# Squares of x at eight late steps, input weights tied behind the last key/value copy, and four smaller moves in a hybrid attention layer

## The chip, the cores and the metric

One core of a Trainium2 chip. The time is device microseconds of one execution, as the median of several runs. The engines are TensorE (PE: matmuls, and PEld: their weight loads), VectorE (DVE), ScalarE (ACT), GpSimd (POOL), and SyncE (SP), which here only issues DMAs. Each engine takes its instructions in one fixed order and waits at the head of its queue.

## The reference

One encoder layer on x of 1024 positions by 1024 channels, float32. Two groups of attention heads read one projection; a gated convolutional feed-forward follows.

```python
hn = rms_norm(x, norm1_g)
proj = hn @ w_in                  # [qA 512 | kA 128 | vA 128 | qB 512 | kB 512 | vB 512]
qa = apply_axial_rope(rms_norm(qa, qa_norm_g), tables)
ka = apply_axial_rope(rms_norm(ka, ka_norm_g), tables)
out_a = global_gqa_attention(qa, ka, va)                # dense, 8 query and 2 kv heads
out_b = dilated_mixture_attention(rms_norm(qb, qb_norm_g), rms_norm(kb, kb_norm_g), vb)
mixed = concatenate([rms_norm(out_a, outa_norm_g), rms_norm(out_b, outb_norm_g)])
x = x + mixed @ w_out
x = x + conv_ffn(rms_norm(x, norm2_g), w_up, conv_w, conv_b, w_down)
```

`rms_norm` divides by the root of the mean of squares, so the squares of all of x are needed before a value of the projection can be scaled. `dilated_mixture_attention` is three patterns of strided windows for eight heads.

## The kernel before

All operands lie in two large SBUF areas (`bigf` for plain float32, `bigr` for the rounded parts that go to the PE) and one PSUM area (`ps`); the profile names only these three. A float32 product is made of three matmuls of 512 columns: high by high, high by low, low by high (L461 to L463). So each operand is first split: a high part by an ACT copy, and the low part by a DVE subtraction (`split`, L261 and L262, for x and its sums; `w_prep`, L446 to L450, for weights).

The stages follow one another on the PE: the input projection (to about 185 us of the trace), dense attention of group A (16 groups g of heads and positions, to about 388 us), the dilated heads of group B, the output projection, the up-projection with its convolution, and the down-projection.

**Projection.** First the key and value columns of group A: eight tiles of positions (`kv_proj`), four PSUM banks in turn, each copied out of its bank by ACT (`kv_out`, L335) and stored. Then 14 products (two halves of the columns, each as a seven-product scheme of 2 x 2 blocks, in the order 1, 5, 2, 3, 6, 7, 4 and 1, 5, 2, 6, 7, 4, 3), each over four slices k: 56 units m, and `in_unit(m)` issues twelve matmuls. Products 3, 5, 6, 7 take sums of blocks of x, which `x_sum` (DVE, L290 to L294) makes and `s_split` splits. `w_prep(m + 4)` stands behind unit m; its parts go to a ring of six buffers, so a weight's high copy waits for the PE to be done with the weight six places ahead.

**Mean of x.** `n_load` loads a tile of 128 rows of x (512 KB) into one buffer, `F_ROPE`; `n_sq` squares it on ACT with a running sum (L300). There is one such buffer, so a load can start only when the square before it is done. Behind the eighth square, `mean_x` makes the norm's factor. The key heads of group B are then normed, in two sets of four tiles (`done("kb", 0, u)` and `done("kb", 4, u)`): a square on ACT (L523; the first set's square goes to `F_ROPE`, the second's to part of the query area), a sum over each head on DVE (L526), a root, its refinement on DVE, a product (L541), and a store to `kscr`.

**Dense attention.** For each g and each pair of key blocks the PE makes scores (L796, L797), ACT takes the exponential (L802), ACT or DVE copies the high part (L806, L804), DVE subtracts for the low part (L807), and the PE multiplies by the values (L781). Between them stand steps of other work by a table `spread` (which g, which step): the rotary steps of the remaining query heads (`roped`; POOL L544 and L549, DVE L554 and L557) and the norms of group B's queries (`rest`, with the square at L577). By g, too, the first dilated heads' keys are loaded (`load_k`, from `kscr`), split (`b_split_k`, ACT L901 and POOL L902), and the outputs scaled (`scale_load` L835, `scale_a` L838).

**Dilated heads.** For each head, over 4 steps of a counter n: scores (L1038, L1039), DVE and ACT work around them (L1047, L1051), then `b_move`, two SP DMAs that put a head's outputs into the layout for the norm (L1087).

**What sets the order.** A scheduler gives each engine its queue from program order and dependences. `tc.issue_after(ins)` lets the instructions made inside it stand, on the engine of `ins`, only behind `ins`. It binds nothing on other engines. `last_exp`, `last_low` and the new `kv_last` are such instructions.

Of the kernel before, what the change touches and what calls it, by code (L numbers as in the profile page):

```python
# [15 lines left out]
AF = mybir.ActivationFunctionType  # L16
# [132 lines left out]
def tile_encoder_layer(ctx, tc, x, xT, w_in, w_kv, consts, norm2_g, w_out, w_up, convs,  # L149
# [17 lines left out]
    def emit(bounded):  # L167
# [32 lines left out]
        def bank(i, n=512, o=0):  # L200
            return PS[:, 512 * i + o:512 * i + o + n]
# [113 lines left out]
        def kv_bank(tt):  # L315
            return tt % 4
# [15 lines left out]

        def kv_out(i):
            stg = f(F_UA + 256 * i if i < 4 else F_W[1] + 1536 + 256 * (i % 2), 256)
            act(stg, bank(kv_bank(i), 256), AF.Copy)  # L335
            dma(kvscr[i], stg)

        def k4(o, j, n=64, off=0):
            return fp(o + 128 * j + off, [1024, 4], [64, 2], [1, n])
# [428 lines left out]
        def a_main_bounded(g, prep, tail, late, plan, late_plan):  # L768

            b, kv = grp(g)  # L770
            q2 = R_Q2A + 512 * (g % 2)
            ob = 6 + g % 2
            slots = {}

            def pv(j):
                ph, pl = slots[j]
                for u in range(2):
                    kt = 2 * j + u
                    v = R_VA + 132 * kt + 66 * kv
                    for i, (w, p) in enumerate(((v, ph), (v + 1056, ph), (v, pl))):  # L780
                        mm(bank(ob)[0:66], r(w, 66), r(p + 512 * u, 512), start=(kt == 0 and i == 0), stop=(kt == 7 and i == 2))  # L781

            def last():
                pv(3)
                vec.tensor_copy(f(F_OT, 512)[0:66], bank(ob)[0:66])
                for u in range(2):
                    dma(f(qab(b) + 256 * kv, 256)[64 * u:64 * u + 64].rearrange("p (c n) -> p c n", c=2),
                        fp(F_OT + 128 * u, [256, 2], [1, 128])[0:64])
                    dma(dna[u:u + 1, b, 256 * kv:256 * kv + 256].rearrange("o (c n) -> o c n", c=2),
                        fp(F_OT + 128 * u, [256, 2], [1, 128])[64:65])  # L790

            for j in range(4):
                st = 2 * (j % 2)
                for u in range(2):
                    kt = 2 * j + u
                    mm(bank(st + u), r(R_K2A + 1024 * kv + 128 * kt, 128), r(q2, 512), start=True, stop=False)  # L796
                    mm(bank(st + u), r(R_KHA + 1024 * kv + 128 * kt, 128), r(q2, 512), start=False, stop=True)  # L797
                n = pairs[0]
                pairs[0] += 1
                p, ph, pl = F_PB[n % 3], R_PHB[j], R_PLB[j]  # L800
                slots[j] = ph, pl
                last_exp[0] = act(f(p, 1024), bank(st, 1024), AF.Exp).ins  # L802
                if j == 1:
                    vec.tensor_copy(r(ph, 1024), f(p, 1024))  # L804
                else:
                    act(r(ph, 1024), f(p, 1024), AF.Copy)  # L806
                last_low[0] = vec.tensor_tensor(r(pl, 1024), f(p, 1024), rf(ph, 1024), op=OP.subtract).ins  # L807
                for kt in (2 * j, 2 * j + 1):
                    take(prep, plan[kt])
                    take(late, late_plan[kt])  # L810
                    now = f(F_PB[(n - 1) % 3], 1) if 0 < kt < 7 and g > 1 else \
                        rf(R_Q2A + 512 * ((g + (kt == 7)) % 2), 1)
                    for step in spread.pop((g, kt), []):
                        step(now)
                step = tail.pop(0) if tail else None
                if step:
                    step()
                if j > 2:
                    pv(j - 3)

            return [lambda: pv(1), lambda: pv(2), last]
# [520 lines left out]
        def at(m, fn, *a):  # L1342
            steps[m].append(lambda: fn(*a))

        for i in range(2, 8):
            at((4, 5, 7, 8, 10, 11)[i - 2], n_sq, i)
            if i < 7:
                at((4, 5, 7, 8, 10, 11)[i - 2], n_load, i + 1)
        at(11, mean_x)
        at(18, dma, f(F_ROPE, 1024), rope)  # L1350
        at(5, dma, f(O_OG, 240), convs)
# [35 lines left out]
        for m in range(4 * len(prods)):  # L1387
            c, n = prods[m // 4]
            if m < 52:
                in_unit(m)  # L1390
            else:
                for k in range(4):
                    in_unit(52 + k, [m - 52])
                in_out(13, m - 52)
                in_last = nc.cur_bb.bb.instructions[-1]
            if m % 4 == 3 and m < 52:
                for t in range(4):
                    in_out(m // 4, t)
            if m == 2:
                for i in range(4):  # L1400
                    kv_tile(i)
            if m == 3:
                for i in range(4, 8):
                    kv_tile(i)
                    if i % 2:
                        n_sq(i // 2 - 2)
                        n_load(i // 2 - 1)
            w_prep(m + 4)
            for s in steps.pop(m, []):
                s()  # L1410
        assert not steps
# [5 lines left out]
        if bounded:  # L1417

            def hold(o, now):
                vec.scalar_tensor_tensor(f(o, 1), now, 0.0, f(o, 1), op0=OP.mult, op1=OP.add)  # L1420

            def run(ts, o=None):
                def at(now):
                    if o is not None:
                        hold(o, now)
                    with tc.issue_after(in_last):
                        for t in ts:
                            t()
                return [at]

            tick = [lambda now: vec.tensor_copy(f(F_KN[0], 1), now)]
            for ts, at in zip(roped, (((0, 2), (1, 4), (1, 6)), ((2, 2), (3, 2), (3, 4)), ((3, 6), (4, 4), (4, 6)))):
                spread[at[0]] = tick + run(ts[:-2])
                spread[at[1]] = run(ts[-2:-1], F_KN[0])
                spread[at[2]] = run(ts[-1:], F_RS)
            for i, d in enumerate(rest):
                square_at, mean_at, root_at, refine_at, norm_at, gain_at = done(*d, i)
                spread[5 + i, 2] = [square_at]
                spread[5 + i, 7] = [mean_at]
                if i == 3:  # L1440
                    spread[9, 3] = [root_at]
                    spread[9, 7] = [refine_at]
                spread[10 + i, 0] = [norm_at]
                spread[11 + i, 2] = [gain_at]
        else:
            for s in sum(roped + [done(*d) for d in rest], []):
                s()
# [5 lines left out]
        if not bounded:  # L1453
# [5 lines left out]
        tail = []  # L1459
        prep = []  # L1460
        SM_A, SM_B = SM_T, SM_T + 64
        dense_late = {8: [(recip_load, 0)], 9: [(recip, 0), (scale_load, 0), (scale_load, 1), (scale_load, 2)],
                      11: [(scale_a, 0), (scale_load, 3)], 12: [(squares, 0, 0, 0, 0), (scale_a, 1)],
                      13: [(squares, 1, 0, 0, 1), (scale_a, 2)], 14: [(squares_sum, (0, 1), 0, SM_A), (squares, 2, 0, 0, 2), (scale_a, 3)],
                      15: [(squares, 3, 0, 0, 3)]}
        for g in range(16):

            prep += a_prep(g + 1) if g < 15 else []
            if g == 14:
                prep += [lambda: b_split(0)] + sum(sum(b_prep(0), []), [])  # L1470
            plan = {0: (1, 0, 1, 0, 0, 0, 0, 0), 14: (1, 1, 1, 0, 0, 0, 1, 1), 15: (1, 1, 0, 1, 0, 0, 0, 0)}.get(g, (0, 1, 0, 0, 1, 0, 0, 0)) if bounded else {14: (1, 1, 1, 1, 1, 2, 2, 2), 15: (2, 2, 2, 2, 1, 1, 1, 1)}.get(
                g, (1, 1, 1, 1, 1, 1, 1, 0))
            tail = a_main(g, prep, tail, late, plan, (0, 2, 2, 2, 1, 1, 1, 1))
# [10 lines left out]
            if g == 9:  # L1484
                load_tee(0, 0)
                load_tee(0, 1)
                load_tmx(1)
            if bounded:
                for fn, *a in dense_late.get(g, []):
                    with tc.issue_after(last_exp[0] if fn is squares else last_low[0]):  # L1490
                        fn(*a)
            if g == 11:
                load_k(0)
            if g == 13:
                load_k(1)
            if g == 10 and bounded:
# [49 lines left out]
        def dilated():  # L1546
# [11 lines left out]
            for n in range(32 + 4):  # L1558
# [14 lines left out]
                        b_recip(6)  # L1573
                    wo_load(5)
                h1, i1 = divmod(n - 7, 4)
                if h1 >= 0 and i1 == 0:
                    b_move(h1)
                h1, i1 = divmod(n - 3, 4)
                if 0 <= n - 3 < 32:
# [10 lines left out]
                if n < 32:  # L1590
# [19 lines left out]
                        step(1, "k0")  # L1610
                    for a, k in (((1, "k1"),), ((1, "q0"), (2, "split_k")), ((1, "q1"), (2, "split_q")), ((2, "k0"),))[i]:
                        step(h + a, k)
                    if n == 3:
                        for c, v in ((64, 1.0), (130, 0.0)):
                            fill(rp(R_VBB[1] + c, [132, 8], [1, 2]), 8, 2, v)
# [9 lines left out]
                if n == 34:  # L1625
                    with tc.issue_after(copied[0]):
# [1 line left out]
                    newton(f(SM_A + 16, 8), f(SM_A, 8), f(SM_A + 8, 8), f(SM_A + 24, 8))  # L1628

        dilated_late = {3: [(squares_sum, (2, 3), 0, SM_A)], 4: [(recip_load, 1)], 8: [(recip, 1)], 9: [(scale_load, 4)], 10: [(scale_load, 5)], 11: [(scale_load, 6)],  # L1630
                        13: [(scale_a, 4)], 14: [(scale_a, 5), (scale_a, 6)], 15: [(scale_load, 7)],
                        18: [(squares, 4, 0, 1, 0), (scale_a, 7)], 21: [(squares_sum, (4,), 1, SM_A)],
                        22: [(squares, 5, 0, 1, 0), (scale_b, 0)], 25: [(squares_sum, (5,), 1, SM_A)],
                        26: [(squares, 6, 0, 1, 0)], 29: [(squares_sum, (6,), 1, SM_A), (mix_split, 0, 0)],
# [660 lines left out]
```

## Time and profile before

| | us |
|---|---|
| three runs | 1169.40, 1170.62, 1173.34; median 1170.62 |
| profiled execution, own time | 1171.02 |
| its span in the trace | 1169.1 |
| PE busy in 0 to 50 / 50 to 160 / 160 to 240 | 47.33 / 110.00 / 78.20 |
| PE busy in 240 to 400 / 400 to the end | 158.92 / 763.39 |

The profiled execution's own time is 1.9 us more than its span, for what lies ahead of the first and behind the last instruction. The trace gives for each instruction its start, its length, its line and, in brackets, how long its engine sat idle before it and what ended that. Lengths of one engine's neighbours overlap a little, since a start is taken before its predecessor has fully drained.

### The profile page before, as it was taken

The numbers are of one execution on the slowest core, as the hardware profiler recorded it, in microseconds if no ns is written. First come the engines' busy times: TensorE is split into PE (matmuls) and PEld (weight loads), VectorE is DVE, ScalarE is ACT, GpSimd is POOL, SyncE is SP. The second block draws the span as 40 slices with busy tenths as digits, with TensorE's granted clock in tenths as the row PEclk, the third lists the DMA queues.
The fourth block names the chain that finished last, engine by engine and source line by source line (L and its number), as shares of the span: only waits on it lengthen the run. The fifth ranks groups of instructions, "written<-read, shape, count | busy, mean of one in ns | idle before, by whom it ended". The sixth has DMA issues, their size and how long they took to land.

```text
span 1169.1 us, 16273 instructions
## 1 busy us (share of the span) xinstructions
PE 1157.8 (99%) x5736; PEld 954.6 (82%) x5736; DVE 1014.4 (87%) x1367; ACT 657.3 (56%) x970; POOL 329.1 (28%) x239
## 2 busy tenths in 40 slices
PE   9999999999999999999999999999999999999998
PEld 8888887666679998887888888888888888888886
DVE  7969888899998897689999999999999996966573
ACT  6975738799898866346443435344434453533331
POOL 0000222510033410121555655564656503000000
PEclk9999999999999999999999999999999999999999
DMA  9566220122135966342232323233232359968862
GB/s 305 180 183 152 77 67 17 37 64 62 36 90 143 214 173 190 108 135 73 64 117 81 117 96 112 100 107 108 98 125 86 109 198 324 333 204 256 295 223 77
DMA packets 130791, 161.85 MB, mean 138 GB/s; under 512 B 47568, under 2 KB 84112, under 8 KB 130576
## 3 DMA queue, kind: packets, MB, share of 16 engines
q1 hardware_dynamic: 128272, 154.73, 41.7%
q0 software_dynamic: 2144, 5.77, 2.2%
q8 instruction: 46, 0.75, 0.3%
q10 hardware_dynamic: 288, 0.26, 0.1%
q14 instruction: 41, 0.34, 0.1%
HBM read 117.86 MB, written 33.91 MB: 130 GB/s over the span
## 4 chain that ended last, share of the span: by engine, by line
PE 52%; DVE 1%; ACT 0%; issue 0%
PE ps L1771 11%; PE ps L1770 11%; PE ps L1769 11%; PE ps L1913 6%; PE ps L1912 6%; PE ps L1914 6%; DVE bigr L2099 0%; DVE bigf L1902 0%; DVE bigr L1740 0%; DVE bigr L2149 0%; DVE bigf L2136 0%; ACT bigr L2095 0%; DVE bigf L2151 0%; DVE bigr L2148 0%; DVE bigf L1728 0%; DVE bigf L2134 0%
## 5 line engine op out<-in xcount | busy, mean ns | idle before, releaser
L1771 PE MATMUL ps<-bigr 128*128 128x512 f32 x616 | 239.9, 389 | 0.6 <-DVE bigr L1740 0.6
L1769 PE MATMUL ps<-bigr 128*128 128x512 f32 x616 | 239.8, 389 | 0.0
L1770 PE MATMUL ps<-bigr 128*128 128x512 f32 x616 | 239.7, 389 | 0.0
L1809 DVE SCALAR_TENSOR_TENSOR bigf<-bigf 128x768 f32<-128x768 f32 (+1 forms) x176 | 192.8, 1132 | 0.7
L1736 ACT ACTIVATE bigr<-bigf 128x512 fp32r<-128x512 f32 x154 | 92.0, 623 | 138.4 <-POOL bigf L1724 108.3
L1892 ACT ACTIVATE bigr<-bigf 128x1024 fp32r<-128x1024 f32 (+1 forms) x99 | 83.9, 868 | 115.3 <-PE ps L1914 82.0
L1771 PEld LDWEIGHTS ps<-bigr 128*128 128x128 f32 x616 | 115.6, 188 | 25.1 <-DVE bigr L1740 1.2
L1770 PEld LDWEIGHTS ps<-bigr 128*128 128x128 f32 x616 | 115.6, 188 | 24.2
L1769 PEld LDWEIGHTS ps<-bigr 128*128 128x128 f32 x616 | 115.6, 188 | 23.8
L1893 DVE TENSOR_TENSOR bigr<-bigf,bigr 128x1024 fp32r<-128x1024 f32 (+1 forms) x99 | 96.6, 995 | 28.5 <-ACT bigr L1892 25.1
L1913 PE MATMUL ps<-bigr 128*128 128x512 f32 x308 | 119.8, 389 | 0.0
L1912 PE MATMUL ps<-bigr 128*128 128x512 f32 x308 | 119.8, 389 | 0.0
L1914 PE MATMUL ps<-bigr 128*128 128x512 f32 x308 | 119.8, 389 | 0.0
L1740 DVE TENSOR_TENSOR bigr<-bigf,bigr 128x512 fp32r<-128x512 f32 x112 | 105.7, 944 | 1.5 <-ACT bigr L1736 0.9
L781 PE MATMUL ps<-bigr 128*66 128x512 f32 x384 | 100.4, 394 | 0.6 <-DVE bigr L807 0.6
L461 PE MATMUL ps<-bigr 128*128 128x512 f32 x224 | 87.6, 391 | 1.5 <-ACT bigf L335 1.5
L462 PE MATMUL ps<-bigr 128*128 128x512 f32 x224 | 87.2, 389 | 0.0
L463 PE MATMUL ps<-bigr 128*128 128x512 f32 x224 | 87.2, 389 | 0.0
L807 DVE TENSOR_TENSOR bigr<-bigf,bigr 128x1024 fp32r<-128x1024 f32 x64 | 81.3, 1275 | 4.0 <-ACT bigr L806 3.2
L1774 DVE TENSOR_TENSOR bigf<-ps,bigf 128x512 f32<-128x512 f32 x110 | 74.9, 680 | 4.8 <-PE ps L1771 4.7
L781 PEld LDWEIGHTS ps<-bigr 128*66 128x66 f32 x384 | 51.1, 136 | 31.5 <-DVE bigr L807 1.1
L1740 POOL TENSOR_TENSOR bigr<-bigf,bigr 128x512 fp32r<-128x512 f32 x42 | 66.3, 1579 | 29.7 <-ACT bigr L1736 28.7
(252 smaller groups left out, 2346.7 us busy)
## 6 DMA issues: line engine op xcount, KB each, us to landing
bigf<-w_down SPq DMA_DIRECT2D x99, 256.0 KB
bigf<-w_up SPq DMA_DIRECT2D x44, 512.0 KB
bigf<-gscr SPq DMA_DIRECT2D x77, 256.0 KB
gscr<-bigf SPq DMA_DIRECT2D x31, 512.0 KB
bigf<-x SPq DMA_DIRECT2D x16, 512.0 KB
bigf<-w_in SPq DMA_DIRECT2D x31, 256.0 KB
bigf<-w_out SPq DMA_DIRECT2D x8, 512.0 KB
bigr<-bigr POOLq DMA_DIRECT2D x16, 256.0 KB, 4.2
```

The lines of the kernel that those rows point to most:

```text
L461: mm(o, r(a, 128), r(w, 512), start=(k == 0 and n != 2 and (c == 1 or n != 3)), stop=False, skip_group_check=True)
L781: mm(bank(ob)[0:66], r(w, 66), r(p + 512 * u, 512), start=(kt == 0 and i == 0), stop=(kt == 7 and i == 2))
L1736: act(rp(R_OP[m % 6], [128, 4], [1, 128]), wu_src(m), AF.Copy)
L1740: low = lambda eng: eng.tensor_tensor(rp(o + 512, [128, 4], [1, 128]), src, rfp(o, [128, 4], [1, 128]), op=OP.subtract)
L1769: mm(bank(b), wh, th, start=(k == 0 and n in (1, 5, 6, 7)), stop=False, skip_group_check=True)
L1770: mm(bank(b), wh, tl, start=False, stop=False, skip_group_check=True)
L1771: mm(bank(b), wl, th, start=False, stop=(k == 3), skip_group_check=True)
L1809: vec.scalar_tensor_tensor(f(a + o, n), f(i + d, n), w_, f(a + o, n), op0=OP.mult, op1=OP.add)
L1893: vec.tensor_tensor(r(d + 1024 + i, w), f(src, w), rf(d + i, w), op=OP.subtract)
L1912: mm(o, ah, r(d, 512), start=(q == 0 and n in (1, 5, 2)), stop=False, skip_group_check=True)
L1913: mm(o, ah, r(d + 1024, 512), start=False, stop=False, skip_group_check=True)
L1914: mm(o, al, r(d, 512), start=False, stop=(q == NQ - 1), skip_group_check=True)
```

## The change

The `n_sq` steps stood at m = 3 (two) and at 4, 5, 7, 8, 10, 11; they now stand at m = 4 to 11, one each, behind the last key/value copy on ACT. `w_prep` from m = 3 on is put behind the same copy, also on ACT alone (its DVE parts follow by dependence). In the dense stage the high copy of the very first pair goes to DVE; the third rotary set stands two steps to four steps later; the square of the first query norm stands two steps later; `load_k(0)` is asked for at g = 5 in place of 11, and its split, `b_split_k(0)`, at g = 6, behind the last exponential, in place of g = 14. Two `b_move` (heads 2 and 3) stand three counts of n later, and the scaling of the seventh tile of group A stands one n later.

```diff
         def kv_out(i):
...
-            act(stg, bank(kv_bank(i), 256), AF.Copy)
+            kv_last[0] = act(stg, bank(kv_bank(i), 256), AF.Copy).ins
...
-                if j == 1:
+                if j == 1 or g + j == 0:
                     vec.tensor_copy(r(ph, 1024), f(p, 1024))
...
-        for i in range(2, 8):
-            at((4, 5, 7, 8, 10, 11)[i - 2], n_sq, i)
+        def n_sq_late(i):
+            with tc.issue_after(kv_last[0]):
+                n_sq(i)
+
+        for i in range(8):
+            at(4 + i, n_sq_late, i)
             if i < 7:
-                at((4, 5, 7, 8, 10, 11)[i - 2], n_load, i + 1)
+                at(4 + i, n_load, i + 1)
...
                 for i in range(4, 8):
                     kv_tile(i)
-                    if i % 2:
-                        n_sq(i // 2 - 2)
-                        n_load(i // 2 - 1)
-            w_prep(m + 4)
+            if m > 2:
+                with tc.issue_after(kv_last[0]):
+                    w_prep(m + 4)
+            else:
+                w_prep(m + 4)
...
-            for ts, at in zip(roped, (((0, 2), (1, 4), (1, 6)), ((2, 2), (3, 2), (3, 4)), ((3, 6), (4, 4), (4, 6)))):
+            for ts, at in zip(roped, (((0, 2), (1, 4), (1, 6)), ((2, 2), (3, 2), (3, 4)), ((3, 6), (4, 6), (5, 0)))):
...
-                spread[5 + i, 2] = [square_at]
+                spread[5 + i, 2 + 2 * (i == 0)] = [square_at]
...
-        dense_late = {8: [(recip_load, 0)], 9: [...],
+        dense_late = {6: [(b_split_k, 0)], 8: [(recip_load, 0)], 9: [...],
...
-                prep += [lambda: b_split(0)] + sum(sum(b_prep(0), []), [])
+                prep += [lambda: (b_split_q if bounded else b_split)(0)] + sum(sum(b_prep(0), []), [])
...
+            if g == (5 if bounded else 11):
+                load_k(0)
             if bounded:
                 for fn, *a in dense_late.get(g, []):
-                    with tc.issue_after(last_exp[0] if fn is squares else last_low[0]):
+                    with tc.issue_after(last_exp[0] if fn in (squares, b_split_k) else last_low[0]):
                         fn(*a)
-            if g == 11:
-                load_k(0)
...
-                if h1 >= 0 and i1 == 0:
+                if h1 >= 0 and i1 == 0 and h1 not in (2, 3):
                     b_move(h1)
...
+                    if n in (18, 22):
+                        b_move(n // 4 - 2)
...
-                        13: [(scale_a, 4)], 14: [(scale_a, 5), (scale_a, 6)], 15: [(scale_load, 7)],
+                        13: [(scale_a, 4)], 14: [(scale_a, 5)], 15: [(scale_load, 7), (scale_a, 6)],
```

The new lines shift the numbers behind them by two in the projection and the dense stage: L446 becomes L448, L449 L451, L523 L525, L541 L543, L475 L477.

ACT around the last key/value copy, before: L335 are the copies out of the banks, L300 the squares of x, L446 and L449 the weights' high copies, L434 and L437 scaled weights, L261 the splits of x and its sums.

```order
30 L335 ACTIVATE bigf<-ps 128x256
31 L434 ACTIVATE bigf<-bigf 128x512
32 L335 ACTIVATE bigf<-ps 128x256
33 L261 ACTIVATE bigr<-bigf 128x512
34 L446 ACTIVATE bigr<-bigf 128x512
35 L300 ACTIVATE bigf<-bigf 128x1024
36 L449 ACTIVATE bigr<-bigf 128x512
37 L335 ACTIVATE bigf<-ps 128x256
38 L446 ACTIVATE bigr<-bigf 128x512
39 L261 ACTIVATE bigr<-bigf 128x512 x4
40 L335 ACTIVATE bigf<-ps 128x256
```

The same place on ACT now.

```order
31 L335 ACTIVATE bigf<-ps 128x256
32 L261 ACTIVATE bigr<-bigf 128x512 x3
33 L335 ACTIVATE bigf<-ps 128x256
34 L261 ACTIVATE bigr<-bigf 128x512 x5
35 L335 ACTIVATE bigf<-ps 128x256
36 L436 ACTIVATE bigf<-bigf 128x512
37 L448 ACTIVATE bigr<-bigf 128x512
38 L300 ACTIVATE bigf<-bigf 128x1024
39 L451 ACTIVATE bigr<-bigf 128x512
40 L448 ACTIVATE bigr<-bigf 128x512 x2
41 L261 ACTIVATE bigr<-bigf 128x512
42 L439 ACTIVATE bigf<-bigf 128x512
```

Squares and weights left the rows ahead of the last copy, and eight splits of x and its sums moved ahead of it in their place. The first square of x (row 26 before, not shown) is now row 38.

DVE between the first and second square of the first key norms, before: the rows of 8 and of 16 elements and L400, L401 are small steps of `mean_x`, the root and its refinement, L541 is the product of the norm, L443 and L450 are weight steps.

```order
84 L443 SCALAR_TENSOR_TENSOR bigf<-bigf 128x512
85 L224 SCALAR_TENSOR_TENSOR bigf<-bigf 128x8
86 L222 TENSOR_TENSOR bigf<-bigf 128x16
87 L400 COPY bigf<-bigf 128x1
88 L450 TENSOR_TENSOR bigr<-bigf,bigr 128x512
89 L223 SCALAR_TENSOR_TENSOR bigf<-bigf 128x16
90 L401 COPY bigf<-bigf 128x8
91 L224 SCALAR_TENSOR_TENSOR bigf<-bigf 128x16
92 L541 TENSOR_TENSOR bigf<-bigf 128x4x256
```

The same steps now.

```order
84 L223 SCALAR_TENSOR_TENSOR bigf<-bigf 128x8
85 L222 TENSOR_TENSOR bigf<-bigf 128x16
86 L224 SCALAR_TENSOR_TENSOR bigf<-bigf 128x8
87 L223 SCALAR_TENSOR_TENSOR bigf<-bigf 128x16
88 L402 COPY bigf<-bigf 128x1
89 L224 SCALAR_TENSOR_TENSOR bigf<-bigf 128x16
90 L403 COPY bigf<-bigf 128x8
91 L543 TENSOR_TENSOR bigf<-bigf 128x4x256
```

One L443 and one L450 no longer stand between the small steps and the product.

ACT around the squares of the second key norms (L523), before; L348 are squares of group A's keys, L532 the root.

```order
95 L446 ACTIVATE bigr<-bigf 128x512
96 L449 ACTIVATE bigr<-bigf 128x512 x2
97 L348 ACTIVATE bigf<-bigf 128x4x128
98 L523 ACTIVATE bigf<-bigf 128x4x256
99 L348 ACTIVATE bigf<-bigf 128x4x128
100 L449 ACTIVATE bigr<-bigf 128x512
101 L532 ACTIVATE bigf<-bigf 128x16
102 L449 ACTIVATE bigr<-bigf 128x512
103 L523 ACTIVATE bigf<-bigf 128x4x256
```

The same place now, where these squares are L525.

```order
92 L448 ACTIVATE bigr<-bigf 128x512
93 L451 ACTIVATE bigr<-bigf 128x512 x3
94 L350 ACTIVATE bigf<-bigf 128x4x128
95 L451 ACTIVATE bigr<-bigf 128x512
96 L525 ACTIVATE bigf<-bigf 128x4x256
97 L350 ACTIVATE bigf<-bigf 128x4x128
98 L448 ACTIVATE bigr<-bigf 128x512
99 L534 ACTIVATE bigf<-bigf 128x16
100 L479 ACTIVATE bigf<-ps 128x512 x4
101 L448 ACTIVATE bigr<-bigf 128x512
102 L525 ACTIVATE bigf<-bigf 128x4x256
```

Counted from the start of ACT's queue, 34 weight copies (L446 and L449) stood ahead of the first of these two squares and 36 ahead of the second; now it is 36 and 38.

More of the change, by code (lines that the diff above doesn't have):

```diff
@@ L334, in kv_out @@
             stg = f(F_UA + 256 * i if i < 4 else F_W[1] + 1536 + 256 * (i % 2), 256)
-            act(stg, bank(kv_bank(i), 256), AF.Copy)
+            kv_last[0] = act(stg, bank(kv_bank(i), 256), AF.Copy).ins
             dma(kvscr[i], stg)
+        kv_last = [None]
         def k4(o, j, n=64, off=0):
@@ L1461, in emit @@
         SM_A, SM_B = SM_T, SM_T + 64
-        dense_late = {8: [(recip_load, 0)], 9: [(recip, 0), (scale_load, 0), (scale_load, 1), (scale_load, 2)],
+        dense_late = {6: [(b_split_k, 0)], 8: [(recip_load, 0)], 9: [(recip, 0), (scale_load, 0), (scale_load, 1), (scale_load, 2)],
                       11: [(scale_a, 0), (scale_load, 3)], 12: [(squares, 0, 0, 0, 0), (scale_a, 1)],
```

## The prediction

> **What bounds the kernel now.** I read the page first, then the waits by engine, then the rows of the stages that the change touches.
>
> ```profile
> span 1169.1 us, 16273 instructions
> PE 1157.8 (99%) x5736; PEld 954.6 (82%) x5736; DVE 1014.4 (87%) x1367; ACT 657.3 (56%) x970; POOL 329.1 (28%) x239
> PEclk9999999999999999999999999999999999999999
> ```
>
> The PE is busy for 1157.8 of 1169.1 us, at full clock in every slice. So the time is that of the PE's matmuls, whose number the change leaves alone, plus the stretches in which the PE stands still. Those the waits of the PE list:
>
> ```profile
> PE ps L461 <- ACT bigf L335: 1.5, 1, 1.5
> PE ps L607 <- POOL bigf L605: 1.2, 1, 1.2
> PE ps L796 <- ACT bigf L802: 1.2, 3, 0.5
> PE ps L1038 <- DVE bigf L1047: 0.9, 1, 0.9
> PE ps L781 <- DVE bigr L807: 0.6, 1, 0.6
> PE ps L1771 <- DVE bigr L1740: 0.6, 1, 0.6
> ```
>
> Columns: total, times, longest. They sum to 6.0 us, 0.5% of the time. That is the most that any reordering can win here; what it can lose has no such limit, since every engine's queue is fixed and a late step on ACT or DVE holds up a PE that otherwise never waits. So I look for places where the change brings a PE operand later than the PE wants it. I make the sum against the profiled execution's own 1171.02 us (span 1169.1), 0.4 above the median of 1170.62.
>
> **A. The last key/value copy: 0.** The 1.5 us wait is for the copy below; the tie clears ACT of one square and several weight copies ahead of it.
>
> ```profile
> 33.41 1.05 ACT L300 ACTIVATE bigf<-bigf 128x1024 f32<-128x1024 f32 x1
> 40.97 2.18 ACT L261 ACTIVATE bigr<-bigf 128x512 fp32r<-128x512 f32 x4
> 43.05 0.36 ACT L335 ACTIVATE bigf<-ps 128x256 f32<-128x256 f32 x1
> 34.00:50.00 16.00, 14.51 (x88) 12.66 (x87) 15.69 (x26) 15.06 (x31) 0.00 (x0) 1.00 0.61 197
> ```
>
> But nine splits (L261) now stand among ACT's last rows before the copy, where five did, and each needs a sum of x from DVE, which the window row (PE, PEld, DVE, ACT, POOL busy) shows at 15.69 of 16 us. So DVE, not ACT, now times the copy: it has four more sums to make, and the weights' low parts that go with the tied copies drop out, about as many. The splits end near where they did, at 43.05. Bounds: -1.5 if DVE's order lets the copy come early, +0.5 (a split, 2.18/4) if one more is late. I take 0.
>
> **B. The chain from the squares to product 7: +4.6.** The first square moves from 33.41 to behind the last copy and two ACT rows (L436, L448): 43.05 + 0.36 + 2 x 0.54 = 44.5 us, **11.1 later** (0.54, a quarter of the L261 row's 2.18, is what such a 128x512 row takes of ACT). The rest of the squares cannot hurry:
>
> ```profile
> L300 ACT ACTIVATE bigf<-bigf x8: 1054/1060/1064, 33.4 to 69.7; 128x1024 f32<-128x1024 f32 x8
>   DMA bigf<-x: 6.4, 6
> L297 SPq DMA_DIRECT2D bigf<-x x7: 327/328/333, 34.6 to 66.0; - x7
> 69.68 1.06 ACT L300 ACTIVATE bigf<-bigf 128x1024 f32<-128x1024 f32 x1 [0.60 <-DMA bigf<-x]
> ```
>
> There is one buffer, so square, load, square: (69.68 - 33.41)/7 = 5.18 us a round. Six of the seven rounds end in a wait for the load, so the load sets the pace (66.0 to 69.68, 3.7 us from issue to square), and moving the whole series moves its end by the same 11.1, to 80.8. Behind it hang, in ACT's order then and now, the first key norms and three splits of product 7's sums:
>
> ```profile
> 74.90 0.74 DVE L443 SCALAR_TENSOR_TENSOR bigf<-bigf 128x512 f32<-128x512 f32 x1
> 75.85 0.69 DVE L450 TENSOR_TENSOR bigr<-bigf,bigr 128x512 fp32r<-128x512 f32 x1
> 78.19 1.06 ACT L523 ACTIVATE bigf<-bigf 128x1024 f32<-128x1024 f32 x1 [0.44 <-DVE bigf L541]
> 79.16 1.66 ACT L261 ACTIVATE bigr<-bigf 128x512 fp32r<-128x512 f32 x3
> 85.78 0.39 PE L461 MATMUL ps<-bigr 128*128 128x512 f32 x1
> ```
>
> The first split ends at 79.16 + 0.55 = 79.7, and the PE wants it at 85.78: 6.1 us in hand. The chain loses 11.1 of it, and wins back the two DVE steps that no longer stand in it (0.74 + 0.69 = 1.4). Split done at 89.4, a PE stall of **3.6**. The squares also meet other ACT work on their new places (L439, with its own weight load, stands behind the first): the six waits average 1.1 us, so a square held by one copy more than before loses up to 1.0 from the round. I count that, since such a row does stand there: **+4.6**; bounds 0 (below, rival 3) and 6.
>
> **C. The second key norms: +4.5.** ACT's order now has two more weight copies ahead of each square of the second set. Weight copies are paced there by the PE, one per unit of twelve matmuls:
>
> ```profile
> 108.17 1.06 ACT L523 ACTIVATE bigf<-bigf 128x1024 f32<-128x1024 f32 x1
> 112.49 0.63 ACT L449 ACTIVATE bigr<-bigf 128x512 fp32r<-128x512 f32 x1 [1.03 <-PE ps L463]
> 113.00:176.40 63.40, 63.40 (x291) 52.52 (x290) 56.01 (x96) 34.93 (x65) 14.07 (x22) 1.00 0.30 78
> 163.46 1.23 DVE L554 TENSOR_TENSOR bigf<-bigf 128x1024 f32<-128x1024 f32 x1 [3.29 <-POOL bigf L549]
> 174.79 2.47 DVE L475 TENSOR_TENSOR bigf<-ps,bigf 128x512 f32<-128x512 f32 x4
> 176.38 0.46 PE L207 MATMUL ps<-bigr 128*128 128x128 f32 x4
> ```
>
> The square moves from 108.17 to behind the copy at 112.49: 112.49 + 0.54 = 113.0, **4.85 later** than the PE's own shift. From it hang the norm's DVE steps and, in DVE's and POOL's queues behind them, group A's keys and the rotary steps up to the last in_out additions (L475) and the transposes that read them. Reserve at the end: the second of four L475 ends at 174.79 + 2 x 0.62 = 176.0, the PE's L207 wants its operand at 176.38, about **0.3**. Between, DVE has 63.40 - 56.01 = 7.4 us idle, 3.29 of it a wait for POOL (L549), itself downstream of the same steps. If all idle time took up the delay, C would cost 0; if none, 4.85 - 0.3 = 4.5. DVE's idle time lies mostly behind its late inputs and moves with them, so I take 4.5; bounds 0 and 8 (the POOL wait doubled as well).
>
> **D. Dense attention's start: +1.2.**
>
> ```profile
> 188.09 0.70 DVE L804 CAST bigr<-bigf 128x1024 fp32r<-128x1024 f32 x1 [0.78 <-ACT bigf L802]
> 231.56 1.21 DVE L557 TENSOR_TENSOR bigf<-bigf 128x1024 f32<-128x1024 f32 x1
> 233.70 0.63 ACT L901 ACTIVATE bigr<-bigf 128x512 fp32r<-128x512 f32 x1 [3.28 <-DMA bigf<-kscr]
> 236.70 1.06 ACT L577 ACTIVATE bigf<-bigf 128x1024 f32<-128x1024 f32 x1 [0.36 <-DMA bigf<-vscr]
> ```
>
> The first high copy on DVE spares the 0.6 of L781's wait. The split L901 waits 3.28 us on ACT for the keys' load, with the exponentials (L802) queued behind it; loaded one group ahead and placed behind an exponential, that goes, worth on the PE at most its longest L802 wait, 0.5. Against that, the third rotary set now ends (L557, 1.21) next to the first query square (L577, 1.06), which moves less than it: the square must wait for the rotary set's buffer, and the exponentials wait behind the square, as they did behind L901. I price that at both instructions, 2.3: 2.3 - 0.6 - 0.5 = **+1.2**; bounds -2.3 (the waits L607, L781 and L796's longest all go, no new one) and +3.3 (a wait as long as L901's).
>
> **E. The seventh tile's scaling: -0.9.**
>
> ```profile
> 379.08 2.60 SPq L1087 DMA_DIRECT2D bigf<-bigf  x2
> 381.72 1.27 SPq L835 DMA_DIRECT2D bigr<-rna  x2
> 387.18 1.53 DVE L838 TENSOR_TENSOR bigf<-bigf,bigr 128x512 f32<-128x512 f32 x1 [1.14 <-DMA bigr<-rna]
> 388.64 1.21 DVE L1047 TENSOR_TENSOR bigf<-ps,bigf 128x1024 f32<-128x1024 f32 x1
> ```
>
> DVE waits 1.14 for the factors' load, whose issue stands behind the two moves (2.60 on SP), and L1047 behind it holds the PE 0.9. With the scaling behind L1047 and the later moves out of SP's way the wait goes: **-0.9**; bounds -0.9 and +0.9 (the same wait under the next L1047). The moves' four DMAs land three counts later, long before the norm of group B reads them, and the remaining edit (the query part of the first split alone at g = 14) only drops work that has been done earlier: 0 for both, covered by a stage in which ACT has 160 - 142.46 us free:
>
> ```profile
> 240.00:400.00 160.00, 158.92 (x1004) 125.70 (x1003) 147.04 (x192) 142.46 (x192) 33.13 (x31) 1.00 0.39 95
> ```
>
> Without that cover they would cost an ACT copy, 0.6. Sum: 0 + 4.6 + 4.5 + 1.2 - 0.9 = **+9.4**, so 1171.02 + 9.4 = 1180.4.
>
> **The rivals.**
> 1. *C is absorbed.* A PE that stalls 4.6 us in B gives DVE and ACT as much free time, and DVE has 7.4 idle after. Then only B, D and E: +4.9, **1175.9**. Against it: the squares' places depend on the PE's pace, so they shift with it.
> 2. *The clock drops* during B's wait, three times any of before, and the matmuls behind it run slow for a while. The loss can be anything from 0 to the length of the wait (as if it were served twice); the middle, 2.3, gives **1182.7**. Against it stands the end of the trace: the last matmul ends near 1164.15, and the granted clock (third number from the end) is still full 4 to 5 us later.
>
> ```profile
> 1160.00:1180.00 20.00, 4.15 (x19) 3.11 (x17) 2.73 (x4) 0.00 (x0) 0.00 (x0) 0.96 0.15 54
> 1168.00:1169.10 1.10, 0.00 (x0) 0.00 (x0) 0.00 (x0) 0.00 (x0) 0.00 (x0) 1.00 0.00 0
> ```
>
>    The Trainium skill (TensorE: Matmul & The Clock Gate, section HAM oscillation) has matmul gaps of more than about 3.4 us drop the clock to half, until a busy stretch as long has passed: by it B would cost 1.7 us more, an estimate. This trace's end held full clock for longer than that page's gap, so I give the rule little weight.
> 3. *Not slower: the loads of x are quicker on their new place.* They now run from 44.5 on, past the busiest part of the DMA queues. If a round took 5.18 - 4.6/7 = 4.5 us or less, the series would end 4.6 us earlier and B be 0; that 0.7 must come out of a load of 3.7. The first norms are then on time, DVE has its idle 7.4 us undisturbed for C's 4.5, and D + E is +0.3: **1171.3**. The Trainium skill (DMA: Bandwidth & Descriptors, section Anatomy of one DMA — SWDGE (gpsimd) path) fits 2.0 us plus bytes over 436 GB/s, for transfers issued from GpSimd, an estimate of 3.2 us for these 512 KB; the trace's 3.7 is 0.5 above it, less than the 0.7 that this rival needs.
> 4. *The dense start is worse*, at the top of D's bounds: **1182.5** to 1184.
> 5. *The tie does what its words suggest*: the last copy comes early and A's 1.5 goes, the rest as forecast: **1178.9**. And if the squares' rounds were also hidden, as in 3, the end would be 1169.8.
>
> **How the numbers follow.** Chances: forecast 0.54 (its own range 1177 to 1184), rival 1 0.17, rival 2 0.08, rival 3 0.08, rival 4 0.06, rival 5 0.07. Differences under 0.3%, 3.5 us, a measurement of this kernel cannot tell from none, so "same" is 1167.5 to 1174.5. Faster needs 3 and 5 together with D's lower bound: 0.03. Same is what is left of rival 3 and the low end of rival 1: 0.09. Slower is the rest, 0.88. The range leaves out rival 3 and the upper tails: 1174.5 to 1186.
>
> **What would show it.** In the trace of after: the first L300 near 44.5 and the eighth near 81; a PE wait of 3 to 6 us at about 86, ended by ACT L261; L525 of the second set at about 113 plus that wait; PE waits near 160 to 185 of some 4 us in all; no wait of L901 for `kscr`; the PE's wait for L1049 gone. Wrong would be: squares closer than 5 us apart, no PE wait near 86, or clock digits under 9.

## The result, and the profile after

The changed kernel takes 1179.26 us (median of six runs, 1178.36 to 1180.12) where the kernel before takes 1170.53 (six runs): a ratio of 1.0074, 95% interval 1.0064 to 1.0084. That is 0.7% slower, 1.1 us under the forecast of 1180.4. The profiled execution took 1179.02, its span 1177.2 us, 8.1 more than before.

First the page of the changed kernel, then the PE's waits (total, times, longest).

```profile
span 1177.2 us, 16273 instructions
PE 1160.1 (99%) x5736; PEld 955.7 (81%) x5736; DVE 1015.8 (86%) x1368; ACT 657.2 (56%) x969; POOL 327.2 (28%) x239
```

```profile
PE ps L463 <- ACT bigr L261: 5.2, 1, 5.2
PE ps L798 <- ACT bigr L714: 1.7, 3, 0.7
PE ps L207 <- DVE bigf L477: 1.2, 1, 1.2
PE ps L609 <- POOL bigf L607: 1.2, 1, 1.2
PE ps L1040 <- DVE bigf L1049: 0.8, 1, 0.8
PE ps L463 <- ACT bigr L386: 0.8, 1, 0.8
PE ps L1780 <- DVE bigr L1749: 0.6, 1, 0.6
```

Two things stand out. The list of waits has one of 5.2 us at its head, and the PE, with the same 5736 matmuls, is 2.3 us longer at work: some matmuls ran slower. Both are in one place. The ACT and PE rows there:

```profile
41.33 0.37 ACT L335 ACTIVATE bigf<-ps 128x256 f32<-128x256 f32 x1
42.83 1.05 ACT L300 ACTIVATE bigf<-bigf 128x1024 f32<-128x1024 f32 x1
80.57 1.06 ACT L300 ACTIVATE bigf<-bigf 128x1024 f32<-128x1024 f32 x1 [0.68 <-DMA bigf<-x]
88.76 1.66 ACT L261 ACTIVATE bigr<-bigf 128x512 fp32r<-128x512 f32 x3
...
89.43 0.80 PE L463 MATMUL ps<-bigr 128*128 128x512 f32 x1 [5.22 <-ACT bigr L261]
90.03 0.63 PE L464 MATMUL ps<-bigr 128*128 128x512 f32 x1
93.44 0.59 PE L464 MATMUL ps<-bigr 128*128 128x512 f32 x1
93.86 0.40 PE L465 MATMUL ps<-bigr 128*128 128x512 f32 x1
```

The first square starts at 42.83 (33.41 before), the eighth at 80.57 (69.68), the splits of product 7's sums at 88.76 (79.16), and the PE waits for the first of them. Ten matmuls then start from 89.43 to 93.44 and the eleventh at 93.86, 0.44 us apart; from there on they are 0.23 apart. The windows of the same stretch give the granted clock (third number from the end):

```profile
84.20:87.00 2.80, 0.01 (x1) 0.00 (x0) 2.35 (x13) 1.28 (x4) 0.00 (x0) 1.00 0.13 35
87.00:93.80 6.80, 4.37 (x10) 3.47 (x11) 6.80 (x15) 3.25 (x6) 0.00 (x0) 0.50 0.69 178
```

The clock halved 2.8 us after the last matmul and stayed so until 93.8, well into the new work. The loss is 93.86 - 89.43 - 10 x 0.2265 = 2.2 us (0.2265 us is the spacing of these matmuls at full clock).

By place, from the two traces: the wait at the last key/value copy gone, -1.5; the new wait, +5.2; the slow matmuls, +2.2; the waits for L386 near 169 us and for L477 near 184 us, +0.8 and +1.2; dense attention's waits changed kind but not sum; the scaling's wait 0.8 in place of 0.9. Together +7.8, of a span longer by 8.1.

### The profile page after: what moved, and what is told of

The parts are those of the page before. It is cut to its first block, busy times and chain, and to the rows that moved or that the text cites. A ratio compares the mean times of both kernels' runs of the same rounds, so it can differ in the third digit from the quotient of the medians.

```text
span 1177.2 us, 16273 instructions
## 1 busy us (share of the span) xinstructions
PE 1160.1 (99%) x5736; PEld 955.7 (81%) x5736; DVE 1015.8 (86%) x1368; ACT 657.2 (56%) x969; POOL 327.2 (28%) x239
## 4 chain that ended last, share of the span: by engine, by line
PE 52%; DVE 1%; ACT 0%; issue 0%
PE ps L1780 11%; PE ps L1779 11%; PE ps L1778 11%; PE ps L1923 6%; PE ps L1921 6%; PE ps L1922 6%; DVE bigr L2108 0%; DVE bigf L1911 0%; DVE bigr L1749 0%; DVE bigr L2158 0%; DVE bigf L2145 0%; ACT bigr L2104 0%; DVE bigf L2160 0%; DVE bigf L1737 0%; DVE bigf L2151 0%; DVE bigr L2157 0%
```

## The experiments

Theory 1: the late squares cost the time, by a chain of one-buffer loads that ends in product 7's splits, with the slow clock behind the wait. Theory 2: the weights tied behind the last copy cost it. All ratios are against runs of the kernel before on the same chip, with 95% intervals.

**Squares back, weights tied.** `n_sq` as in the kernel before, the rest as changed:

```diff
-        for i in range(8):
-            at(4 + i, n_sq_late, i)
+        for i in range(2, 8):
+            at((4, 5, 7, 8, 10, 11)[i - 2], n_sq, i)
...
                     kv_tile(i)
+                    if i % 2:
+                        n_sq(i // 2 - 2)
+                        n_load(i // 2 - 1)
```

> The changed kernel, with the squares of x back at their eight old places and without their tie; the weights stay tied behind the last key/value copy. Theory 1 (the late squares cost the time): the PE's wait of 5.2 us at 84 us and the slow clock behind it go, 7.3 us less: about 1172 us; the wait of 1.5 us at the last copy may come back if a square stands ahead of it (1173). Theory 2 (the tied weights cost it): no change, about 1179, with a long PE wait still near 84 us.

Measured: 1169.14 us, ratio 0.9988 (0.9979 to 0.9998). The long wait and the slow clock are gone. The waits of its PE begin with

```profile
PE ps L798 <- ACT bigr L714: 1.6, 3, 0.7
PE ps L609 <- POOL bigf L607: 1.2, 1, 1.2
```

so the late squares carry the whole loss. The time is 3 us below the 1172 expected: the waits for L386 and L477 of the changed kernel (0.8 and 1.2) went as well, but for 0.2. The rest of the change gains 0.12%, just outside what the runs can tell from nothing.

**Weights free, squares late.**

```diff
-            if m > 2:
-                with tc.issue_after(kv_last[0]):
-                    w_prep(m + 4)
-            else:
-                w_prep(m + 4)
+            w_prep(m + 4)
```

> The changed kernel with the weights free again, the squares of x still late and tied. Theory 1 (late squares): the long PE wait before product 7 stays, 4 to 6 us, the clock drops behind it, and the 1.5 us at the last copy come back: 1179 to 1181 us. Theory 2 (tied weights): the long wait goes, about 1171 us.

Measured: 1177.88 us, ratio 1.0058 (1.0041 to 1.0075). Its longest PE wait:

```profile
PE ps L463 <- ACT bigr L261: 3.6, 1, 3.6
```

Theory 2 falls: without the tie on the weights the wait and the slow clock stay. The expectation missed in three things: the time is 1.1 us under its range, the wait of 3.6 is under its 4 to 6, and the 1.5 us at the last copy did not come back. So moving the squares is enough to clear that copy, without the tie on the weights.

**The wait filled with matmuls.** 23 added matmuls repeat an operand of the first unit of product 7 into the bank that its second block clears; they add work and leave the result as it is.

```diff
                 o = bank(in_bank(c, n) + t)
+                if (c, n, k, t) == (0, 7, 0, 1):
+                    for _ in range(23):
+                        mm(o, r(a_op(n, 0), 128), r(w, 512), start=True, stop=False, skip_group_check=True)
```

> The changed kernel with 23 matmuls of 512 columns added on the PE at the place of its 5.2 us wait, into a bank that the next matmul clears. They take 23 x 0.2265 = 5.2 us. If the clock drops because the PE stands still (theory 1), it stays full, the ten matmuls behind the wait run at 0.2265 instead of 0.43 us, and the time falls by about 2.1 us to about 1177 although the PE does more. If the slow stretch has another cause, or the added matmuls only push the work behind them, the time is 1179 or more and matmuls near 90 us stay at 0.43 us.

Measured: 1175.7 us, ratio 1.004 (1.0026 to 1.0054), against the changed kernel's 1.0074. The PE rows:

```profile
84.45 5.38 PE L465 MATMUL ps<-bigr 128*128 128x512 f32 x23
89.66 0.39 PE L466 MATMUL ps<-bigr 128*128 128x512 f32 x1
89.89 0.39 PE L467 MATMUL ps<-bigr 128*128 128x512 f32 x1
```

With 5.2 us more work in the same place the kernel is faster, and the matmuls behind run at full rate. The mean granted clock says the same of every execution: 0.996 to 0.998 in the six of the changed kernel, 0.999 to 1.0 in the five with the wait filled. So it is the standstill that halves the clock. The gain, 3.6 us by the times (1179.26 to 1175.7) and 4.0 by the ratios, is more than the 2.2 of the slow matmuls. In this profile ACT's order differs too (34 weight copies stand ahead of the second key norms in place of 36), and the 0.8 us wait for L386 is gone; the rest is not accounted for.

**Only the first square freed.**

```diff
-            at(4 + i, n_sq_late, i)
+            at(4 + i, n_sq_late if i else n_sq, i)
```

> The changed kernel with only the first of the eight squares freed from its tie, so that it can run ahead of the last key/value copy and the seven rounds of load and square start earlier. Theory 1 with the rounds setting the pace (one buffer, 5.4 us a round): the eighth square comes up to 5 us earlier (about 75 to 77 instead of 80.6 us), the PE wait of 5.2 shrinks under 1.5 us and the clock stays full: 1172 to 1174 us. If the squares' tie as such (seven of eight still tied) or the tied weights matter, less than 2 us are won: 1177 to 1179.

Measured: 1175.31 us, ratio 1.0036 (1.0022 to 1.005); longest PE wait 3.5 us, clock halved behind it, both in the profiled execution, which at 1177.54 us was the slowest of the five. Better than the changed kernel, but short of the 1172 to 1174 expected. The first, second and eighth square:

```profile
35.55 1.09 ACT L300 ACTIVATE bigf<-bigf 128x1024 f32<-128x1024 f32 x1
45.48 1.05 ACT L300 ACTIVATE bigf<-bigf 128x1024 f32<-128x1024 f32 x1
78.58 1.06 ACT L300 ACTIVATE bigf<-bigf 128x1024 f32<-128x1024 f32 x1 [1.19 <-DMA bigf<-x]
```

The first is 7.3 us earlier than in the changed kernel, but the second, still tied, comes 9.9 us behind it, with its load long there (no wait in its row). A chain of rounds starts at its last tied link. From the second on, six rounds take (78.58 - 45.48)/6 = 5.5 us each, about as in the changed kernel: (80.57 - 42.83)/7 = 5.4.

The 2.0 us by which the eighth square is earlier did not reach the PE in this execution: the splits of product 7's sums stand at 88.60, where they stood at 88.76, since the first square of the key norms is only 0.1 us earlier (81.64 in place of 81.75). On ACT, other steps now stand between it and the eighth square, among them a table load of 1.28 us for the root of `mean_x` (L1339), which stood behind it in the changed kernel:

```profile
80.23 1.28 ACT L1339 ACT_TABLE_LOAD   x1
81.64 1.04 ACT L525 ACTIVATE bigf<-bigf 128x1024 f32<-128x1024 f32 x1
88.60 1.66 ACT L261 ACTIVATE bigr<-bigf 128x512 fp32r<-128x512 f32 x3
```

The wait is shorter, 3.5 in place of 5.2, because the PE came there 1.5 us later, 1.0 of it a wait at the last copy. So this run shows where a chain of rounds starts, but not what an earlier eighth square is worth.

**Half the wait filled**, with 11 added matmuls in place of 23.

> The changed kernel with 11 added matmuls (2.5 us) at the place of the 5.2 us wait, so that the PE works on for 2.5 us and then stands still for about 2.7. In the changed kernel the clock fell 2.8 us after the last matmul. If the length of the standstill decides, with about 3 us as the limit, the clock stays full: about 2.1 us less, 1177. If any wait of some us lets it fall, depending on where a window of the chip's own begins, some of the runs or all keep the ten slow matmuls: 1178 to 1179.

Measured: 1177.62 us, ratio 1.0054 (1.0035 to 1.0073). Inconclusive on the limit that it was meant to find: the wait left over was 3.7 us, not 2.7, since the splits came 1.4 us later as well, and part of the work behind it ran at half clock.

**Second key norms asked for sooner**, at m = 27 in place of 29, with the squares late.

```diff
-        for t0, m in ((0, 12), (4, 29)):
+        for t0, m in ((0, 12), (4, 27)):
```

> The changed kernel with the second key norms asked for at m = 27 in place of 29, so that 34 and 36 weight copies stand ahead of their squares on ACT, as before the change, and not 36 and 38. The wait of 5.2 us and the slow clock stay. If step C is right in kind, the PE's waits near 167 us (0.8, for L386) and 182 us (1.2, for L477) go: about 1177 us. If the second norms are late only because the first were, the waits stay: 1179.

Measured: 1177.88 us, ratio 1.0061 (1.004 to 1.0083). Among the waits of its PE:

```profile
PE ps L463 <- ACT bigr L261: 5.9, 1, 5.9
PE ps L207 <- DVE bigf L477: 1.0, 1, 1.0
```

The wait for L386 (0.8) is gone, that for L477 all but unchanged. The run with the wait filled has 34 and 36 copies too and no wait for L386. But neither has the run with only the first square freed, with 36 and 38: so that the two more copies cost the 0.8 us is not shown, and the ratio cannot be told from the changed kernel's 1.0074. The 1.0 to 1.2 for L477 has not been tied to one cause either: the run with early squares shows 0.2 there, every run with late squares 0.8 to 1.2, but so does one profile below with early squares.

**The dense stage's edits alone** on the kernel before (no tie, squares early, moves as before).

> The kernel before with only the dense stage's edits (first high copy on DVE, third rotary set and first query square later, the first dilated keys loaded at g = 5 and split at g = 6). The prediction's step D, +1.2 us: 1172. The trace of the changed kernel, where the dense waits of the PE sum to 3.2 us as before: no change within 0.5 us, about 1171, with the wait for the exponential replaced by one for the copy L712 and the wait for the low part gone.

Measured: 1170.85 us, ratio 0.9999 (0.9988 to 1.0011): no difference. The PE's waits:

```profile
PE ps L1040 <- DVE bigf L1049: 1.7, 1, 1.7
PE ps L798 <- ACT bigr L714: 1.7, 3, 0.7
PE ps L609 <- POOL bigf L607: 1.2, 1, 1.2
PE ps L463 <- ACT bigf L335: 0.9, 1, 0.9
```

The waits for the low part (L781 before) and for the exponential are replaced by 1.7 us for L714, which was 0.2. As much goes as comes.

**The later moves and scaling alone** on the kernel before.

> The kernel before with only the two later moves of heads and the later scaling of the seventh tile. The prediction's step E, -0.9 us: the PE's wait for L1047 near 388 us gone, 1170. The trace of the changed kernel, where 0.8 of that wait is left: within 0.3 us of before.

Measured: 1170.19 us, ratio 0.9993 (0.9983 to 1.0003): no difference that the runs can tell. The wait is still there, 0.7:

```profile
PE ps L1040 <- DVE bigf L1049: 0.7, 1, 0.7
```

DVE's wait for the factors' load is gone, and L1049 starts at 387.76 in place of 388.64, now behind a wait for its own input. But the PE came 0.8 us sooner as well (388.29, 389.05 before), so most of its wait is left:

```profile
387.76 1.23 DVE L1049 TENSOR_TENSOR bigf<-ps,bigf 128x1024 f32<-128x1024 f32 x1 [2.46 <-ACT ps L1041]
```

**The tied weights with the moves, and the tied weights alone**, on the kernel before.

> The kernel before with the tied weights and the later moves of heads and scaling, without the late squares and the dense stage's edits. If the tied weights are what clears the last key/value copy (its wait of 1.5 us goes, and nothing takes its place while the squares are early) and the moves win 0.2 to 0.9, the time is 1168.5 to 1169.5, the same as with the dense edits. If the dense edits carried part of the gain of the run with early squares, it is 1170 or more.

> The kernel before with the tied weights alone. Step A of the prediction took the tie to be worth nothing at the last copy, 1170.6, with a wait of 1.5 us left at 42 us. The changed kernel's trace, in which the last copy stands 1.7 us earlier and the wait is gone: 1.0 to 1.5 us less than before, 1169.2 to 1169.7.

Measured: 1169.75 us, ratio 0.9987 (0.9978 to 0.9996), and 1170.49, ratio 0.9996 (0.9985 to 1.0007). The first is, with the run of early squares, the fastest of the study, by some 0.13%; it needs none of the dense edits, though it lies 0.25 us above the range expected. The tie alone makes no measurable difference, as step A had it and not as the 1169.2 to 1169.7 expected. Of the last copy's wait, 1.0 and 0.6 us are left in their profiles:

```profile
39.69 2.71 ACT L261 ACTIVATE bigr<-bigf 128x512 fp32r<-128x512 f32 x5 [0.32 <-DVE bigf L292]
42.31 0.36 ACT L335 ACTIVATE bigf<-ps 128x256 f32<-128x256 f32 x1
```

These are the rows with the tie alone: the five splits ahead of the copy wait for DVE's sums (L292), and the copy comes 0.7 us earlier than before (43.05). That profile also shows the 1.2 us wait for L477, which the other of the two, with the same order up to there, does not: its fourth square waits 1.92 us for its load of x, 0.69 in the other. Waits of about 1 us in this stage come and go between profiles, and a single one is not evidence.

## Why the prediction was right, and where it was wrong

The time, the sign and the cause were right. The sum came out close partly because errors cancelled:

| step | forecast | measured in the trace |
|---|---|---|
| A, last copy | 0 | -1.5 |
| B, squares to product 7 | +4.6 | +5.2 |
| slow clock behind B (rival 2) | 0 (+2.3 if it came) | +2.2 |
| C, second key norms | +4.5 | +2.0 |
| D, dense start | +1.2 | 0 |
| E, scaling | -0.9 | -0.1 |
| sum | +9.4 | +7.8 (span +8.1) |

**B** held as a chain: first square 42.83 (forecast 44.5), round 5.4 us (5.18), eighth 80.57 (80.8), a PE wait of 5.2 (4.6), and undoing the squares alone took the whole loss away. Rival 3 fell with it: the loads were no quicker on their new place, 5.4 us a round. That its figures came out so close is partly luck. The square's earlier start (1.7) and the longer rounds (7 x 0.2) cancel, so the splits end at 89.3, as in the sum without its 1.0 for longer rounds (89.4, a stall of 3.6). The other 1.5 us of the wait is the PE, which came there that much sooner because A's wait was gone.

**The clock** was given 8 chances in 100 and came. The step that failed is the argument against it: the end of the trace of before kept full clock for 4 to 5 us after the last matmul, and I took that for the length that a standstill may have. It is one sample of a time that varies: in the changed kernel the clock fell 2.8 us after the last matmul, and in five other runs 2.6 to 4.2 us after the wait began (why it varies, the last section shows). The rule of the Trainium skill that I weighed there (TensorE: Matmul & The Clock Gate, section HAM oscillation: a gap of more than about 3.4 us) was nearer for this wait of 5.2 us, and its price of 1.7 us, an estimate, too: 2.2 were lost. The price from rows, the middle between nothing and the wait, 2.3, was right.

**C** was right in kind and sized too large. The square did move as worked out (118.89 here; 108.17 before, so 10.7, of which the PE itself is 5.9 late (-1.5 + 5.2 + 2.2), leaving 4.8, forecast 4.85). But DVE's four L475, now L477, start at 183.33 in place of 174.79, 8.5 later: DVE's idle time took up 2.2 of it, where I had said that it would move with its late inputs. The 4.5 was the price without that cover, and only 2.0 was paid.

```profile
118.89 1.04 ACT L525 ACTIVATE bigf<-bigf 128x1024 f32<-128x1024 f32 x1
183.33 2.48 DVE L477 TENSOR_TENSOR bigf<-ps,bigf 128x512 f32<-128x512 f32 x4
```

**A** failed as a term: I said that DVE would time the copy as late as before. It came 1.7 us earlier and the PE's wait went, as rival 5 had it; but nothing was won, since the PE only waited longer in B. Moving the squares is enough to clear the copy: in five profiles with all squares late the wait is 0 to 0.2 us, in seven with squares ahead of the copy 0 to 1.5 (0 in the run with squares back and weights tied, so that a share of the tie is not excluded), and with the tie alone DVE's sums do hold the splits as forecast.

**D** named a wait that did not come: the exchange of waits at the dense start is even. The run of these edits alone shows no change. **E** priced a wait as gone that stays: behind the wait for the factors' load, which did go, L1049 waits for its own input, 0.7 to 0.8 us of the PE's wait are left, and the run alone cannot be told from before.

## What to carry to other kernels

Where a series of loads goes through one buffer, its end is its start plus a fixed number of rounds, and what hangs on the end has only the reserve that the trace shows: moving the start by more than that reserve costs the difference, on any engine. Look for the link that was moved last, since freeing one before it wins little. And where the PE is busy throughout, price a new wait of some us not at its own length but at that plus the slow matmuls behind it.

## What the runs showed of the hardware that was not expected

The clock halves behind waits shorter than I had thought, and at no fixed time after they begin. With the dense edits alone, a wait of 1.7 us near 388 us was enough in the profiled execution: the PE worked again from 389.70, and the clock still fell at 390.87 and stayed at half to 394.28. It fell once more behind the last matmul, at 1169.10 (clock third from the end).

```profile
387.46:390.87 3.41, 1.74 (x18) 1.60 (x16) 3.38 (x4) 2.98 (x6) 1.13 (x3) 1.00 0.66 139
390.87:394.28 3.41, 3.41 (x23) 3.41 (x22) 3.11 (x4) 2.40 (x4) 2.44 (x3) 0.50 0.99 240
394.28:1169.10 774.82, 770.41 (x3655) 644.57 (x3654) 670.13 (x831) 352.40 (x512) 258.23 (x153) 1.00 0.46 151
1169.10:1170.40 1.30, 0.00 (x0) 0.00 (x0) 0.00 (x0) 0.00 (x0) 0.00 (x0) 0.50 0.00 0
```

The same wait at 0.7 to 1.0 us in other profiles left the clock full. The changed kernel's trace, cut at its own two falls:

```profile
83.62:87.03 3.41, 0.59 (x3) 0.17 (x1) 2.90 (x14) 1.85 (x5) 0.00 (x0) 1.00 0.13 32
87.03:93.86 6.83, 4.43 (x10) 3.47 (x11) 6.83 (x15) 3.25 (x6) 0.00 (x0) 0.50 0.68 176
93.86:1175.88 1082.02, 1072.74 (x5272) 879.47 (x5270) 946.24 (x1225) 588.70 (x839) 326.66 (x233) 1.00 0.43 132
1175.88:1177.20 1.32, 0.00 (x0) 0.00 (x0) 0.00 (x0) 0.00 (x0) 0.00 (x0) 0.50 0.00 0
```

So the clock changes only at the ends of fixed steps of time. In the six profiles with a fall inside the kernel the half clock lasted 3.41 us (two) or 6.82 to 6.83 (four). From that fall to the one behind the last matmul it is 1088.85 us here and with the weights free, 1085.44, 1085.43, 1082.02 and, with the dense edits, 778.23: 319, 319, 318, 318, 317 and 228 times 3.4133. How long after the start of a wait the clock falls, 2.6 to 4.2 us, thus depends on where in such a step the wait begins.

The Trainium skill (TensorE: Matmul & The Clock Gate, section What's actually happening) has the clock set by windows of about 3.4 us that run freely, and these traces agree. It asks for a whole idle window before a fall; here they differ, for in the window that ended in the fall the PE was busy for 0.59 us in the changed kernel and for 1.74 of 3.41 with the dense edits. How little work lets the clock fall, and whether the kind of matmul matters, stays open.

The kernel before can lose its clock too: in 9 of its 57 executions beside these experiments the mean granted clock was 0.997 or 0.998, and these took 1171.4 to 1176.0 us. In which place it fell there, no trace shows.
